# A queue that spreads the transpositions of the attention heads over the long products, and another spacing of the gates in the last attention stage

## The chip, the cores and the metric

One core of a Trainium2 chip runs the whole program. The metric is the device time of one execution in microseconds. The kernel is written with a tile scheduler: the code names tiles and operations, and the scheduler then puts the instructions of each engine in an order, takes buffers from small pools and adds the waits. An instruction that the code emits earlier has the higher priority; it is placed as soon as the scheduler's own reckoning says that its inputs and buffers are ready.

## What is computed

Two layers on a residual stream of 512 tokens by 1024 columns. Each layer mixes the tokens by five branches of four heads, sums them under gates, projects and normalises; then a mixture of 16 experts follows.

```python
h = x @ w_in                              # all q, k, v of the five branches
o_sb, o_moba, o_mla, o_nsa, o_mem = ...   # five attentions, 4 heads of 64 each, (512, 256) out
for i, o in enumerate((o_sb, o_moba, o_mla, o_nsa, o_mem)):
    gate = sigmoid(x @ w_gate[i] + b_gate[i])       # 1024 x 1024 per branch
    merged = merged + gate * (o @ w_br[i])
h = layer_norm(ALPHA * h + merged @ w_out)
h = layer_norm(ALPHA * h + hierarchical_moe(h))     # 16 experts, two per token
```

Every attention is a softmax over at most 512 keys, but for the stick-breaking one (`sb`), which takes a running product along the keys. The native sparse attention (`nsa`) has two such maps per head (selected and window) and a compressed one.

## The kernel before, in words

Products run in a split form: each operand is a high and a low part, and three products of the parts replace one. So a tile of 128 by 512 out of 1024 inputs is 24 products of 512 columns (`fm_tile`, L166), which the text calls long products.

An attention head is a chain for each of its four query blocks of 128 rows. `score_block` multiplies q by k into a PSUM tile `s` (2 banks, L116); VectorE subtracts the distance and takes the minimum (L254) or only the minimum (L257); ScalarE takes the exponent (L259); VectorE inverts the sum and scales (L260, L262, L264). The result lies in an SBUF tile `ne`, of which there are 3. `to_pt` then turns its blocks of 128 columns on TensorE (`tr`, L124) into a PSUM tile `pt` (2 banks), and ScalarE and VectorE copy them, split, into `pth` and `ptl`. These have one buffer each, so a head's tiles must be read before the next head's are written. When four query blocks have been turned, the product with v follows (`causal_pv`, into the one `pv` bank), then the head's output `oo`. A branch's output is split to `oh`, and `gates` uses it. In `sb` the chain from `s` to `ne` is tanh, a running product (L432) and a difference (L433).

`mixer` runs five stages, one for each branch. In each, `weave` draws from up to three generators, in the order that a string gives: `a` is the next score block (or the end of a head), `g` the next half of a gate tile of the branch before (24 long products, or 6 with `w_br`), `q` the next piece of the next branch's q, k and v. When the string is at its end, what is left of each generator runs. After the last stage the gates of the last branch follow alone, and then the output projection and the experts, whose weights are loaded into memory that the attention's tiles have left.

Before, a step `a` emits the score products and, right behind them, the transpositions of the same block, one after another; the end of a head emits its product with v at once. The scheduler keeps that priority: it places the one to four transpositions of a block together, at the moment when its own reckoning says that the softmax is done.

Of the kernel before, what the change touches and what calls it, by code (L numbers as in the profile page):

```python
# [18 lines left out]
P = 128  # L19
# [51 lines left out]
class Trunk:  # L71
    def __init__(self, tc, A, C, out, dbg=None, upto=None):
        self.tc, self.nc, self.A, self.C, self.out = tc, tc.nc, A, C, out
        self.dbg, self.upto = dbg or {}, upto
        self.uid = 0

    def nm(self, s):
        self.uid += 1
# [33 lines left out]
            return e.tensor_tensor(out, in_, hi.bitcast(F32), ALU.subtract)  # L112
        return e.scalar_tensor_tensor(out, in_, scale, hi.bitcast(F32), ALU.mult, ALU.subtract)

    def mm(self, out, lhsT, rhs, start, stop):
        self.nc.tensor.matmul(out, lhsT, rhs, start=start, stop=stop)  # L116

    def mm3(self, out, ah, al, bh, bl, start, stop):
        self.mm(out, ah, bh, start, False)
# [39 lines left out]
    def fm_tile(self, wh, wl, M=P, N=S, x=None, cut=1):  # L159
        o = self.ps("f")  # L160
        xh, xl = (self.xh, self.xl) if x is None else x
        for c in range(cut):
            n = slice(c * N // cut, (c + 1) * N // cut)
            for k in range(KT):
                for m, (a, b) in enumerate(((wh, xh), (wh, xl), (wl, xh))):
                    self.nc.tensor.matmul(o[:M, n], a[:, k, :M], b[:, k, n], start=c + k + m == 0, stop=k == KT - 1 and m == 2,  # L166
                                          skip_group_check=cut > 1)
        return o

    def fm_chunk(self, w, c0, use, n=2, cut=1):  # L170
# [6 lines left out]
    def tm_chunk(self, w, c0, use, x=None, nt=NT, outer="k"):  # L177

        xh, xl = (self.xh, self.xl) if x is None else x
        o = [self.ps("f") for _ in range(nt // 2)]  # L180
        hl = {}

        def part(g, kk, t):
            if g not in hl:
                hl[g] = self.split_w(self.load_w(w[512 * g : 512 * g + 512, c0 : c0 + 256].rearrange("(k p) c -> p k c", p=P), (4, 256)))
            h, l = hl[g]
            k = 4 * g + kk
            sl = slice(t * P, (t + 1) * P)
            d = o[t // 2][:, 256 * (t % 2) : 256 * (t % 2) + 256]
            for m, (a, b) in enumerate(((xh, h), (xh, l), (xl, h))):  # L190

                self.nc.tensor.matmul(d, a[:, k, sl], b[:, kk, :], start=k == 0 and m == 0 and t % 2 == 0,  # L192
                                      stop=k == KT - 1 and m == 2, skip_group_check=True)
# [72 lines left out]

    def to_pt(self, e, nb, dst):

        t = self.ps("pt")
        for b in range(nb):  # L270
            self.tr(t[:, b * P : (b + 1) * P], e[:, b * P : (b + 1) * P])
        src = t[:, : nb * P].rearrange("p (b q) -> p b q", q=P)
        h, l = dst
        self.hi(h, src)
        self.lo(l, src, h)

    def pv_out(self, pv, o32, at):

# [36 lines left out]
    def causal_head(self, passes, vt, strip=0, slope=1.0):  # L315
        pt = self.pt_tiles()
        for i in range(NT):
            L = P * (i + 1)
            e = self.score_block(i, L, passes, self.strip[:, 384 - P * i : 512] if strip == 0 else None, slope, causal=strip == 1)
            self.to_pt(e, i + 1, self.causal_dst(pt, i))  # L320
            yield
        pv = self.ps("pv")
        self.causal_pv(pv, pt, vt, True, True)
        return pv

    def std_passes(self, q, k):

# [45 lines left out]
    def mem_att(self, l, out):  # L373
        for pr in range(2):
            o32 = self.o_tile()
            out.append(o32)
            for hh in range(2):
                h = 2 * pr + hh
                q, k = self.mq[h], self.mk[h]
                pt = self.pt_tiles()  # L380
                for i in range(NT):
                    e = self.score_block(i, MEM, self.std_passes(q, k), None)
                    self.to_pt(e, 2, [t.rearrange("p (c q) -> p c q", q=P)[:, i : i + 5 : 4, :] for t in pt])
                    yield
                pv = self.ps("pv")
                for j in range(2):
                    for m in range(2):
                        self.mm(pv[:, :S], self.mv[j][:, h, :], pt[m][:, 512 * j : 512 * j + 512], j == 0 and m == 0, j == 1 and m == 1)
                self.pv_out(pv, o32, self.H2[hh])
                yield  # L390
            self.dump(f"o_mem{pr}_{l}", o32)

# [17 lines left out]
    def sb_att(self, l, out):  # L410
        nc = self.nc
        for pr in range(2):
            o32 = self.o_tile()
            out.append(o32)
            for hh in range(2):
                h = 2 * pr + hh
                passes = self.std_passes(self.sq[h], self.sk[h])
                pt = self.pt_tiles()
                for i in range(NT):
                    L = P * (i + 1)  # L420
                    s = self.ps("s")
# [12 lines left out]
                    self.to_pt(t, i + 1, self.causal_dst(pt, i))  # L434
                    yield
                pv = self.ps("pv")
                self.causal_pv(pv, pt, lambda j: self.sv[j][:, h, :], True, True)
                self.pv_out(pv, o32, self.H2[hh])
                yield
            self.dump(f"o_sb{pr}_{l}", o32)  # L440

# [14 lines left out]
    def moba_att(self, l, out):  # L456
        for pr in range(2):
            o32 = self.o_tile()
            out.append(o32)
            for hh in range(2):  # L460
                h = 2 * pr + hh
                q, k = self.bq[h], self.bk[h]
                pv = yield from self.causal_head(self.std_passes(q, k), lambda j: self.bv[j][:, h, :], 0, SLOPES[h])
                self.pv_out(pv, o32, self.H2[hh])
                yield
            self.dump(f"o_moba{pr}_{l}", o32)

# [131 lines left out]
    def mla_att(self, l, out):  # L599
        for pr in range(2):  # L600
            o32 = self.o_tile()
            out.append(o32)
            for hh in range(2):
# [6 lines left out]
                pv = yield from self.causal_head(passes, lambda j: self.lv[j][:, h, :], 1)  # L610
                self.pv_out(pv, o32, self.H2[hh])
                yield
            self.dump(f"o_mla{pr}_{l}", o32)

# [104 lines left out]
    def nsa_att(self, l, out):  # L719
# [32 lines left out]
        for pr in range(2):  # L752
            o32 = self.o_tile()
            out.append(o32)
            for hh in range(2):
# [3 lines left out]
                for m in range(2):  # L759
# [7 lines left out]
                pv = self.ps("pv")  # L767
                self.mm(pv, self.vc[:, h, :], pc[:, 0, :], True, False)
                self.mm(pv, self.vc[:, h, :], pc[:, 1, :], False, False)
                for m in range(2):  # L770
                    self.causal_pv(pv, pts[m], lambda j, m=m: self.nv[j][:, m, :], False, m == 1)
                self.pv_out(pv, o32, self.H2[hh])
                yield
            self.dump(f"o_nsa{pr}_{l}", o32)

# [87 lines left out]
            self.hi(h, v)  # L863
            self.lo(self.xl[:, 4 * g : 4 * g + 4, t * P : (t + 1) * P], v, h)

    @staticmethod
    def weave(parts, order):

        for c in order:
            next(parts[c], None)  # L870
        for g in parts.values():
            for _ in g:
                pass

    def start(self, l):

# [719 lines left out]
    def layer(self, l, gat, att):  # L1596
# [8 lines left out]
        with tc.tile_pool(name=f"pre{l}", bufs=1, reuse_waits="tile") as pre:  # L1605
# [6 lines left out]
            with tc.tile_pool(name=f"exp{l}", bufs=1, reuse_waits="tile") as ep:  # L1612
# [30 lines left out]
    qs = "pp"  # L1643
    wq = "ssss"
    rest = 3
    orders = ('aaaqaaaaqaaaaaaaaaaaaqqa', 'gggqqgaaaaggaaaaaaggaaaaqqggggggaqqqqagagaaa', 'qaagaaggagqqaggaaaqaggaqaaaaqggaqqaaaaggqggqqggqq', 'ggqgaaaaaaaaaaagqgaaaggqagggggggqqqqgaaaaga', 'ggaaaaaaaaaggggggggaaaaaaaaaaaaaaaagaaaaaaaaaagggagg')
    x1 = 0

    class _Pool:
# [66 lines left out]
```

## Time and profile before

| | |
|---|---|
| runs | 1702.87, 1696.06, 1697.85 us; median 1697.85 us |
| profiled execution | 1704.54 us, of which the span of instructions is 1702.7 us |
| mean granted TensorE clock | 0.972 of full speed |
| busy share of the span | TensorE 94%, VectorE 74%, ScalarE 51%, GpSimd 16% |
| attention stages | about 45 to 530 us (layer 0) and 885 to 1385 us (layer 1) |

The profiled execution is a little slower than the runs; its rows are used for durations and for who waits. A busy share of TensorE says little by itself, since products overlap: a product of 512 columns is listed with about 0.4 us, but the next starts 0.23 us after it. Where TensorE has to wait, the listed idle time starts only when the last listed product has ended, so a wait costs that overlap on top of the idle time shown.

### The profile page before, as it was taken

What the parts mean: (1) busy time and instruction counts of PE and PEld (TensorE: products, weight loads), DVE (VectorE), ACT (ScalarE), POOL (GpSimd) and SP (SyncE); (2) the same over time, 40 slices, a digit from 0 to 9 for tenths busy, and PEclk for the clock granted to TensorE, in tenths of its full rate; (3) what the DMA queues carried; (4) which work ended last, traced back from release to release, by engine and by line L of the source; (5) the groups of instructions that cost most, each with busy time, mean ns of one, the idle gap of its engine ahead of it and who ended that gap; (6) DMA issues with size and microseconds to landing.
All of it is one profiled execution on the core that took longest, in us unless ns stands there. A gap on an engine that the chain in (4) does not pass through costs nothing. (4 is left out here: it accounts for less than half of the span.)

```text
span 1702.7 us, 22755 instructions
## 1 busy us (share of the span) xinstructions
PE 1603.2 (94%) x7936; PEld 1271.8 (75%) x7936; DVE 1253.3 (74%) x2551; ACT 867.3 (51%) x1655; POOL 272.7 (16%) x218
## 2 busy tenths in 40 slices
PE   8999999999999998899699999999999999989995
PEld 7877877788777786666587778777877787766673
DVE  6777658764785689988788766588557956898887
ACT  5644446343463335788346444464344624358871
POOL 0000011111112112333300000111101121223332
PEclk9999999989999998999799999999999999999997
DMA  8232222434328747997541323223332285499954
GB/s 254 64 91 77 67 71 61 119 95 124 106 79 281 255 165 282 378 379 251 195 141 52 94 73 81 66 62 98 79 88 63 58 305 183 170 326 380 381 178 156
DMA packets 254563, 273.61 MB, mean 161 GB/s; under 512 B 38666, under 2 KB 191360, under 8 KB 254432
## 3 DMA queue, kind: packets, MB, share of 16 engines
q1 hardware_dynamic: 241032, 223.98, 41.3%
q0 software_dynamic: 13312, 47.98, 8.2%
q8 instruction: 67, 1.10, 0.3%
q14 instruction: 64, 0.52, 0.1%
q10 hardware_dynamic: 88, 0.03, 0.0%
HBM read 239.18 MB, written 32.77 MB: 160 GB/s over the span
## 5 line engine op out<-in xcount | busy, mean ns | idle before, releaser
L166 PE MATMUL f<-xh,wh 128*128 128x512 f32 (+2 forms) x1920 | 631.0, 397 | 2.0 <-DVE ot L592 1.1
L166 PEld LDWEIGHTS f<-xh,wh 128*128 128x128 f32 (+1 forms) x1920 | 355.7, 189 | 77.0 <-PE f L625 1.2
L166 PE MATMUL f<-xl,wh 128*128 128x512 f32 (+2 forms) x960 | 381.1, 397 | 0.0
L112 DVE TENSOR_TENSOR wh<-rw,wh 128x1024 fp32r<-128x1024 f32 (+1 forms) x174 | 227.5, 1313 | 51.5 <-ACT wh L97 50.4
L798 POOL TENSOR_TENSOR mg<-mg,gt 128x512 f32<-128x512 f32 x64 | 96.8, 1512 | 986.1 <-DVE gt L797 986.1
L166 PEld LDWEIGHTS f<-xl,wh 128*128 128x128 f32 (+1 forms) x960 | 181.0, 188 | 36.7 <-DVE xl L112 0.2
L97 ACT CAST wh<-rw 128x1024 fp32r<-128x1024 f32 (+3 forms) x178 | 178.5, 1012 | 52.6 <-PE f L192 14.9
L788 ACT ACTIVATE gt<-f,bgh 128x512 f32<-128x512 f32 x80 | 55.0, 688 | 211.8 <-PE f L166 211.8
L116 PE MATMUL f<-wh,xh 128*112 128x512 f32 (+1 forms) x564 | 153.9, 400 | 1.9 <-DVE wh L112 1.9
L116 PE MATMUL f<-oh,bh 128*128 128x512 f32 x480 | 132.5, 403 | 0.1
L797 DVE SCALAR_TENSOR_TENSOR gt<-gt,f 128x512 f32<-128x512 f32 x64 | 43.8, 684 | 107.3 <-PE f L116 102.8
L116 PEld LDWEIGHTS f<-wh,xh 128*112 128x112 f32 (+1 forms) x564 | 98.3, 178 | 31.8 <-DVE wh L112 3.3
L97 ACT CAST pth<-pt 128x128 fp32r<-128x128 f32 (+1 forms) x192 | 77.4, 417 | 87.2 <-PE pt L124 81.5
L116 PE MATMUL f<-eh,xh 128*112 128x512 f32 (+1 forms) x396 | 110.5, 401 | 0.9 <-DVE eh L112 0.8
L112 DVE TENSOR_TENSOR ptl<-pt,pth 128x128 fp32r<-128x128 f32 (+1 forms) x192 | 88.9, 473 | 24.7 <-ACT pth L97 21.8
L116 PEld LDWEIGHTS f<-oh,bh 128*128 128x128 f32 x480 | 89.8, 191 | 20.0 <-issue 1.2
L116 PE MATMUL s<-qk,qk 128*128 128x256 f32 (+7 forms) x416 | 99.2, 336 | 5.9 <-DVE st L254 2.6
L97 ACT CAST wh<-rp 128x1024 fp32r<-128x1024 f32 x84 | 87.5, 1053 | 30.9 <-PE pt L116 16.3
L112 DVE TENSOR_TENSOR wh<-rp,wh 128x1024 fp32r<-128x1024 f32 x70 | 95.4, 1374 | 8.4 <-ACT wh L97 7.8
L124 PE MATMUL pt<-ident,ne 128*128 128x128 f32 x472 | 83.7, 279 | 8.6 <-DVE ne L433 3.8
L116 PEld LDWEIGHTS s<-qk,qk 128*128 128x128 f32 (+1 forms) x416 | 67.5, 194 | 26.9 <-DVE st L254 9.3
L124 PEld LDWEIGHTS pt<-ident,ne 128*128 128x128 f32 x472 | 54.7, 141 | 42.4 <-issue 17.1
(355 smaller groups left out, 2756.4 us busy)
## 6 DMA issues: line engine op xcount, KB each, us to landing
rp<-in_w_up_dram SPq DMA_DIRECT2D x96, 512.0 KB, 14.4
rw<-in_w_gate_dram SPq DMA_DIRECT2D x80, 512.0 KB, 3.8
rp<-in_w_down_dram SPq DMA_DIRECT2D x48, 512.0 KB, 13.6
rw<-in_w_in_dram SPq DMA_DIRECT2D x38, 512.0 KB, 3.8
rw<-in_w_out_dram SPq DMA_DIRECT2D x32, 512.0 KB, 6.5
yd<-xl POOLq DMA_DIRECT2D x28, 448.0 KB, 6.8
xl<-xd POOLq DMA_DIRECT2D x24, 448.0 KB, 7.5
rb<-in_w_br_dram SPq DMA_DIRECT2D x80, 128.0 KB, 3.3
```

Source lines behind the costliest of these rows:

```text
L97: return nc.scalar.copy(out, in_)
L112: return e.tensor_tensor(out, in_, hi.bitcast(F32), ALU.subtract)
L116: self.nc.tensor.matmul(out, lhsT, rhs, start=start, stop=stop)
L124: return self.nc.tensor.transpose(out, in_, self.ident[:k, :k])
L166: self.nc.tensor.matmul(o[:M, n], a[:, k, :M], b[:, k, n], start=c + k + m == 0, stop=k == KT - 1 and m == 2, skip_group_check=cut > 1)
L788: nc.scalar.activation(t, gp, AF.Tanh, bias=self.bgh[:, b * 8 + f : b * 8 + f + 1], scale=0.5)
L797: nc.vector.scalar_tensor_tensor(t, t, 1.0, bp, ALU.add, ALU.mult)
L798: i = nc.gpsimd.tensor_tensor(m, m, t, ALU.add)
```

## The change

`mm` gets a counter: each product of 256 columns or more is a tick. Emission of the turned blocks goes through a queue (`pend`). `to_pt` puts one entry for each block in it; the first may run 20 ticks after it was queued, each following one 2 ticks after the one before, and after the last of a block row there is a gap that fills up to 10 ticks. The entry of the last block also emits the copies into `pth` and `ptl`. The end of a head, with its product with v, is an entry of the same queue, so it comes behind its own transpositions. `tick` runs inside whatever emits long products at that time, so the blocks are emitted singly between the products of gates and projections. `weave` empties the queue at the end of each stage. All products of `fm_tile` and `tm_chunk` now go through `mm`. The fifth order string is another: its sixteen `g` stood in five clusters of 1 to 8; now they stand in pairs with four or five `a` between them.

```diff
+        self.pend, self.now, self.due, self.big = [], 0, 0, None
...
-    def mm(self, out, lhsT, rhs, start, stop):
-        self.nc.tensor.matmul(out, lhsT, rhs, start=start, stop=stop)
+    def mm(self, out, lhsT, rhs, start, stop, **kw):
+        i = self.nc.tensor.matmul(out, lhsT, rhs, start=start, stop=stop, **kw)
+        if rhs.shape[-1] >= self.long:
+            self.big = i
+            self.tick()
+
+
+    def tick(self):
+
+        if self.busy:
+            return
+        self.now += 1
+        while self.pend and max(self.pend[0][0], self.due) <= self.now:
+            if self.do_next():
+                break
+
+    def do_next(self):
+        _, gap, f = self.pend.pop(0)
+        self.busy = True
+        f()
+        self.busy = False
+        self.due = self.now + gap
+        return gap
+
+    def flush(self):
+        while self.pend:
+            self.do_next()
+
+    def later(self, f, gap=0, delay=0):
+
+        self.pend.append((self.now + delay, gap, f))
...
-        t = self.ps("pt")
+        h, l = dst
+        ts = []
+
+        def turn(b):
+            if b == 0:
+                ts.append(self.ps("pt"))
+            t = ts[0]
+            if True:
+                self.tr(t[:, b * P : (b + 1) * P], e[:, b * P : (b + 1) * P])
+            if b == nb - 1:
+                src = t[:, : nb * P].rearrange("p (b q) -> p b q", q=P)
+                self.hi(h, src)
+                self.lo(l, src, h)
         for b in range(nb):
-            self.tr(t[:, b * P : (b + 1) * P], e[:, b * P : (b + 1) * P])
-        src = t[:, : nb * P].rearrange("p (b q) -> p b q", q=P)
-        h, l = dst
-        self.hi(h, src)
-        self.lo(l, src, h)
+            self.later(lambda b=b: turn(b), self.space if b < nb - 1 else max(1, self.gap_t - self.space * (nb - 1)), 0 if b else self.delay)
...
-        pv = self.ps("pv")
-        self.causal_pv(pv, pt, vt, True, True)
-        return pv
+
+        def out(use):
+            pv = self.ps("pv")
+            self.causal_pv(pv, pt, vt, True, True)
+            use(pv)
+        return lambda use: self.later(lambda: out(use))
...
         for g in parts.values():
             for _ in g:
                 pass
+        self.flush()
...
+    busy = False
+    long, delay, space, gap_t = 256, 20, 2, 10
```

The fifth string, before and now:

```text
ggaaaaaaaaaggggggggaaaaaaaaaaaaaaaagaaaaaaaaaagggagg
ggaaaaaggaaaaggaaaaaggaaaaggaaaaaggaaaaggaaaaaggaaaa
```

What the scheduler makes of it is seen in the order of TensorE's instructions. In both programs 472 blocks of the `ne` tiles are turned. Before, they stand in 178 runs, 36 of which are a single transposition; now they stand in 324 runs, 262 of them single.

The first place is on TensorE in layer 0's MoBA stage (`s` is a score, `pt<-ident,ne` a turned block, `f<-xh,wh` and `f<-xl,wh` long products, `f<-oh,bh` the six products with `w_br`). Before:

```order
L166 MATMUL f_2145<-xh_102,wh_2142 128x512 x2
L166 MATMUL f_2145<-xl_103,wh_2142 128x512
L166 MATMUL f_2145<-xh_102,wh_2142 128x512
L124 MATMUL pt_2104<-ident,ne_2098 128x128 x3
L166 MATMUL f_2145<-xh_102,wh_2142 128x512
L166 MATMUL f_2145<-xl_103,wh_2142 128x512
L124 MATMUL pt_2119<-ident,ne_2113 128x128 x4
L166 MATMUL f_2145<-xh_102,wh_2142 128x512 x2
```

Seventeen long products and three transpositions stand between the score of `ne_2113` and its four transpositions. The same score's blocks now (its score is `s_2099`, its blocks are `ne_2104`; L117 and L154 are the new numbers of L116, L166 and L124):

```order
L117 MATMUL f_2132<-xh_102,wh_2129 128x512 x2
L154 MATMUL pt_2161<-ident,ne_2104 128x128
L117 MATMUL f_2132<-xl_103,wh_2129 128x512
L117 MATMUL f_2132<-xh_102,wh_2129 128x512
L154 MATMUL pt_2161<-ident,ne_2104 128x128
L117 MATMUL f_2168<-oh_2043,bh_2124 128x512 x2
L154 MATMUL pt_2161<-ident,ne_2104 128x128
L117 MATMUL f_2168<-oh_2043,bh_2124 128x512
L117 MATMUL f_2168<-oh_2046,bh_2124 128x512
L154 MATMUL pt_2161<-ident,ne_2104 128x128
```

The four blocks stand two long products apart, and 28 long products and five other transpositions stand between the score and the first of them.

The second place is on TensorE in layer 0's last stage (`nsa`), at the first two scores of the second head; that of 256 columns is the one to look at. Before:

```order
L166 MATMUL f_4407<-xh_102,wh_4404 128x512
L116 MATMUL f_4434<-oh_4015,bh_4399 128x512 x3
L116 MATMUL f_4434<-oh_4018,bh_4399 128x512 x3
L116 MATMUL s_4446<-qk_3754,qk_3849 128x128
L116 MATMUL s_4446<-qk_3755,qk_3849 128x128
L116 MATMUL s_4459<-qk_3754,qk_3849 128x256
L116 MATMUL s_4459<-qk_3755,qk_3849 128x256
```

Now:

```order
L154 MATMUL pt_4281<-ident,ne_4139 128x128
L117 MATMUL f_4296<-oh_4015,bh_4248 128x512 x3
L117 MATMUL f_4296<-oh_4018,bh_4248 128x512
L154 MATMUL pt_4301<-ident,ne_4150 128x128
L117 MATMUL f_4296<-oh_4018,bh_4248 128x512 x2
L117 MATMUL s_4312<-qk_3754,qk_3849 128x128
L117 MATMUL s_4312<-qk_3755,qk_3849 128x128
L117 MATMUL s_4321<-qk_3754,qk_3849 128x256
L117 MATMUL s_4321<-qk_3755,qk_3849 128x256
```

The score `s_4321` takes the PSUM bank of `s_4234`. VectorE's reduction of `s_4234` writes the `ne` buffer that held `ne_4150`, and so it waits for the transposition `pt_4301<-ident,ne_4150`, which now stands two long products and two short ones ahead of the score.

## Rows read from the trace of the kernel before

**Rows 1.** Windows of both attention stretches: length, then busy us by engine.
```profile
45.00:530.00 485.00, 474.91 (x2352) 380.30 (x2352) 334.73 (x774) 236.00 (x530) 49.47 (x42) 0.99 0.33 92
885.00:1385.00 500.00, 491.08 (x2453) 393.78 (x2452) 345.83 (x785) 242.35 (x540) 42.74 (x27) 0.99 0.30 84
```

**Rows 2.** Waits of TensorE: waiting line, releaser, total us, times, longest.
```profile
PE pt L124 <- DVE ne L433: 3.8, 12, 0.5
PE pt L124 <- DVE ne L262: 2.8, 6, 0.8
PE s L116 <- DVE st L254: 2.6, 6, 0.8
PE s L116 <- ACT ne L259: 1.7, 2, 1.4
PE s L116 <- ACT ne L427: 0.8, 2, 0.4
PE pt L124 <- DVE st L260: 0.6, 2, 0.3
PE pt L124 <- DVE ne L264: 0.4, 2, 0.3
```

**Rows 3.** Timeline of TensorE in MoBA: start, us, engine, line, tiles, count, idle.
```profile
213.85 0.39 PE L166 MATMUL f<-xl,wh 128*128 128x512 f32 x1
215.03 0.63 PE L124 MATMUL pt<-ident,ne 128*128 128x128 f32 x4 [0.80 <-DVE ne L262]
```

**Rows 4.** Timeline of VectorE and GpSimd ahead of that wait.
```profile
210.02 0.69 DVE L254 CUSTOM_DVE_ANT_0 ne<-s,strip 128x512 f32<-128x512 f32 x1
...
212.81 1.40 POOL L798 TENSOR_TENSOR mg<-mg,gt 128x512 f32<-128x512 f32 x1 [212.38 <-DVE gt L797]
213.05 1.44 DVE L112 TENSOR_TENSOR bh<-rb,bh 128x256 fp32r<-128x256 f32 x1
214.41 0.47 DVE L262 TENSOR_SCALAR ne<-ne,st 128x512 f32<-128x512 f32 x1
```

**Rows 5.** Timeline of TensorE: one transposition between long products.
```profile
961.80 0.39 PE L166 MATMUL f<-xh,wh 128*128 128x512 f32 x1
962.03 0.27 PE L124 MATMUL pt<-ident,ne 128*128 128x128 f32 x1
962.06 0.48 PE L166 MATMUL f<-xh,wh 128*128 128x512 f32 x1
962.38 0.39 PE L166 MATMUL f<-xl,wh 128*128 128x512 f32 x1
```

**Rows 6.** Timeline of TensorE: four transpositions in a run that waited for nothing.
```profile
280.29 0.40 PE L166 MATMUL f<-xh,wh 128*128 128x512 f32 x1
280.53 0.60 PE L124 MATMUL pt<-ident,ne 128*128 128x128 f32 x4
...
281.20 0.39 PE L166 MATMUL f<-xl,wh 128*128 128x512 f32 x1
```

**Rows 7.** Timeline of TensorE in the latent stage: a score that waited.
```profile
340.39 0.79 PE L116 MATMUL s<-qk,qk 96*128 96x384 f32 x3 [1.42 <-ACT ne L259]
```

**Rows 8.** Groups by form: products with a branch's output.
```profile
L116 PE MATMUL f<-oh,bh 128*128 128x512 f32 x480 | 132.5, 403 | 0.1
```

**Rows 9.** Windows around a fall of the clock; the third last number is the clock.
```profile
360.00:363.00 3.00, 3.00 (x30) 3.00 (x28) 1.14 (x1) 1.62 (x2) 0.00 (x0) 1.00 0.02 3
363.00:366.00 3.00, 3.00 (x13) 2.68 (x13) 0.92 (x6) 0.52 (x4) 0.00 (x0) 0.53 1.10 219
...
369.00:373.00 4.00, 4.00 (x10) 3.14 (x11) 2.22 (x9) 1.91 (x9) 0.36 (x1) 0.50 0.04 8
```

**Rows 10.** Timeline: loads after the attention, and the output projection's first products.
```profile
518.01 1.82 SPq L1329 DMA_DIRECT2D rp<-in_w_up_dram  x3
...
554.45 6.31 SPq L137 DMA_DIRECT2D rw<-in_w_out_dram  x2
...
577.91 0.97 PE L116 MATMUL f<-wh,xh 128*128 128x512 f32 x3
```

More of the change, by code (lines that the diff above doesn't have):

```diff
@@ L165, in fm_tile @@
                 for m, (a, b) in enumerate(((wh, xh), (wh, xl), (wl, xh))):
-                    self.nc.tensor.matmul(o[:M, n], a[:, k, :M], b[:, k, n], start=c + k + m == 0, stop=k == KT - 1 and m == 2,
-                                          skip_group_check=cut > 1)
+                    self.mm(o[:M, n], a[:, k, :M], b[:, k, n], c + k + m == 0, k == KT - 1 and m == 2, skip_group_check=cut > 1)
         return o
@@ L190, in part @@
             for m, (a, b) in enumerate(((xh, h), (xh, l), (xl, h))):
-                self.nc.tensor.matmul(d, a[:, k, sl], b[:, kk, :], start=k == 0 and m == 0 and t % 2 == 0,
-                                      stop=k == KT - 1 and m == 2, skip_group_check=True)
+                self.mm(d, a[:, k, sl], b[:, kk, :], k == 0 and m == 0 and t % 2 == 0, k == KT - 1 and m == 2, skip_group_check=True)
         its = [(g, kk) for g in range(2) for kk in range(4)]
@@ L384, in mem_att, with end @@
                     yield
[L385 to L389, printed above, removed]
+                def end(h=h, hh=hh, pt=pt, o32=o32):
+                    pv = self.ps("pv")
+                    for j in range(2):
+                        for m in range(2):
+                            self.mm(pv[:, :S], self.mv[j][:, h, :], pt[m][:, 512 * j : 512 * j + 512], j == 0 and m == 0, j == 1 and m == 1)
+                    self.pv_out(pv, o32, self.H2[hh])
+                self.later(end)
                 yield
@@ L435, in sb_att, with end @@
                     yield
-                pv = self.ps("pv")
-                self.causal_pv(pv, pt, lambda j: self.sv[j][:, h, :], True, True)
-                self.pv_out(pv, o32, self.H2[hh])
+                def end(h=h, hh=hh, pt=pt, o32=o32):
+                    pv = self.ps("pv")
+                    self.causal_pv(pv, pt, lambda j: self.sv[j][:, h, :], True, True)
+                    self.pv_out(pv, o32, self.H2[hh])
+                self.later(end)
                 yield
@@ L462, in moba_att @@
                 q, k = self.bq[h], self.bk[h]
-                pv = yield from self.causal_head(self.std_passes(q, k), lambda j: self.bv[j][:, h, :], 0, SLOPES[h])
-                self.pv_out(pv, o32, self.H2[hh])
+                pv = yield from self.causal_head(self.std_passes(q, k), lambda j, h=h: self.bv[j][:, h, :], 0, SLOPES[h])
+                pv(lambda x, o32=o32, hh=hh: self.pv_out(x, o32, self.H2[hh]))
                 yield
@@ L609, in mla_att @@
                           (lambda sl: qb[K, sl], lambda sl: ka[K, sl])]
-                pv = yield from self.causal_head(passes, lambda j: self.lv[j][:, h, :], 1)
-                self.pv_out(pv, o32, self.H2[hh])
+                pv = yield from self.causal_head(passes, lambda j, h=h: self.lv[j][:, h, :], 1)
+                pv(lambda x, o32=o32, hh=hh: self.pv_out(x, o32, self.H2[hh]))
                 yield
@@ L766, in nsa_att, with end @@
                     pts.append(pt)
[L767 to L772, printed above, removed]
+                def end(h=h, hh=hh, pts=pts, o32=o32):
+                    pv = self.ps("pv")
+                    self.mm(pv, self.vc[:, h, :], pc[:, 0, :], True, False)
+                    self.mm(pv, self.vc[:, h, :], pc[:, 1, :], False, False)
+                    for m in range(2):
+                        self.causal_pv(pv, pts[m], lambda j, m=m: self.nv[j][:, m, :], False, m == 1)
+                    self.pv_out(pv, o32, self.H2[hh])
+                self.later(end)
                 yield
@@ L864, in x_tile, with weave @@
             self.lo(self.xl[:, 4 * g : 4 * g + 4, t * P : (t + 1) * P], v, h)
-    @staticmethod
-    def weave(parts, order):
+    def weave(self, parts, order):
         for c in order:
@@ L1645 @@
     rest = 3
-    orders = ('aaaqaaaaqaaaaaaaaaaaaqqa', 'gggqqgaaaaggaaaaaaggaaaaqqggggggaqqqqagagaaa', 'qaagaaggagqqaggaaaqaggaqaaaaqggaqqaaaaggqggqqggqq', 'ggqgaaaaaaaaaaagqgaaaggqagggggggqqqqgaaaaga', 'ggaaaaaaaaaggggggggaaaaaaaaaaaaaaaagaaaaaaaaaagggagg')
+    orders = ('aaaqaaaaqaaaaaaaaaaaaqqa', 'gggqqgaaaaggaaaaaaggaaaaqqggggggaqqqqagagaaa', 'qaagaaggagqqaggaaaqaggaqaaaaqggaqqaaaaggqggqqggqq', 'ggqgaaaaaaaaaaagqgaaaggqagggggggqqqqgaaaaga', 'ggaaaaaggaaaaggaaaaaggaaaaggaaaaaggaaaaggaaaaaggaaaa')
     x1 = 0
```

## The prediction

> **What bounds the kernel now.** I read the windows of the two attention stretches first, since the change touches nothing else. TensorE is listed busy for 474.9 of 485 us in layer 0 and for 491.1 of 500 us in layer 1 [rows 1]; VectorE is next, at about 69% in both. So the attention is bound by the rate of TensorE, and all that any new order can win from listed idle time is 10.1 + 8.9 = 19.0 us. Then I read who TensorE waits for. Transpositions (`pt L124`) wait for the end of the softmax: 3.8 + 2.8 + 0.6 + 0.4 = 7.6 us in 22 waits. Scores (`s L116`) wait for a free bank: 2.6 + 1.7 + 0.8 = 5.1 us in 10 waits [rows 2]. A wait costs more than its idle time: a long product is listed with 0.39 us, but the next one starts 0.23 us after it [rows 5], so 0.16 us of overlap is lost as well. One wait shows it: from 213.85 to 215.03 is 1.18 us where 0.23 would do, so 0.95 is lost and 0.80 is shown [rows 3]. With 0.16 for each, transpositions cost 7.6 + 22 x 0.16 = 11.1 us and scores 5.1 + 10 x 0.16 = 6.7 us in the whole program.
>
> The reason for such a wait is a chain that ran slower than it was planned. The score was reduced at 210.02, and its last scaling started at 214.41, because VectorE first had a subtraction for `bh` that took 1.44 us while GpSimd was adding a gate tile [rows 4]. From the start of the score's last product to the first transposition went its own 0.23, 17 long products at 0.23, three transpositions at 0.11 (priced below) and the 0.95 that was lost, together 5.4 us.
>
> **Transpositions singly or in a run.** This is what the change is most visibly about, so I priced it first. One transposition between long products: from 961.80 to 962.38 is 0.58 us, where two long products take 0.46 to 0.47; it adds 0.11 [rows 5]. Four in a run: from 280.29 to 281.20 is 0.91; they add 0.44, which is 0.11 each [rows 6]. So 262 single ones instead of 36 are worth 226 x 0.00 = 0 us. The reason can be seen in the next product's listed 0.48 us: it starts 0.03 us after the transposition but then takes 0.32 until the one after it.
>
> The Trainium skill, on the page "TensorE: Matmul & The Clock Gate" (its opening table of specifications), says that the queue of TensorE is partly reordered, with weight loads pulled ahead of products in flight. By that rule a lone transposition behind a long product would have its weight load covered, and only its own short stream would remain. The rows disagree: two loads fall to one long product there, that of the transposition and that of the product behind it, and the full 0.11 us is paid.
>
> **Waits that go.** The queue moves a transposition away from its score. In the order, counting each product at its pitch in the trace, 138 of 194 block rows had less than 5.4 us of TensorE's work between score and first transposition, the time that the chain took at 215.03; now 35 have. The median distance goes from 4.9 to 8.8 us. At the first place shown under the change there are now 28 long products, 6.4 us, and some transpositions. I take the waits as proportional: 11.1 x 35/138 = 2.8 us remain and 8.3 go. The ends are 11.1 (all go) and 5.5 (half of them have other causes, such as a `pt` bank that is still being copied).
>
> **Waits that come.** A turned block holds its `ne` tile longer, and there are only three. The reduction of a score must wait until its `ne` tile has been turned, and the score after next must wait for the reduction, since there are two banks. In the order, scores that stand less than 1.5 us of TensorE's work behind such a transposition go from 24 to 60. The second place shown is one of them: two long products and two short ones, at most 2 x 0.23 + 2 x 0.11 = 0.68 us, against 0.27 for the transposition [rows 5] and 0.69 for a reduction of 512 columns [rows 4], so 0.28 short. What is queued behind the waiting reduction on VectorE is the other head work and the weights' subtractions; the products that use those are what TensorE would miss next. The lower price is from the waits that can be put on this ring before: `ACT ne L259`, 1.7 + 2 x 0.16 = 2.0 us over 24 places, or 0.08 each, and 36 x 0.08 = 3.0. The upper price is 36 x 0.28 = 10.1; below nothing it can't fall, since a ring that is held longer frees nobody. I take 3.0, as most of the new places are for 128 and 256 columns, where the reduction is shorter and the room just enough.
>
> **What costs nothing, and by which cover.** The branch output's split now comes closer to the products that use it: 2.4 to 2.7 us of TensorE's work from the last product with v in three of five stages, one before. That one stood at 2.4 us and all 480 such products waited 0.1 us in sum [rows 8]; so I price it at nothing, and at 3 us if the cover is gone. The attention's tiles are freed later: the first expert load stands about 12.8 us of TensorE's work later in SP's queue, and the third load for the output projection about 9. In the trace that third load was issued at 554.45 and the projection began at 577.91 [rows 10]; 23 us of room minus 9 still covers it. The gates that were moved in the last stage issue the same loads, casts and adds as before, in pairs; their adds on GpSimd can slow VectorE as at 213.05 [rows 4], but there are no more of them than before.
>
> **The sum.** -8.3 + 3.0 = -5.3 us, 0.3%. The profiled execution took 1704.5 us, so it would be 1699.2 there. The three runs' median is 1697.85, 0.4% less, and on that basis the forecast is 1692.6, rounded to 1693.
>
> **Rivals.** First, the waits go altogether: with the gates spread evenly products are at hand for every stall, and both kinds of waits end, -11.1 - 6.7 = -17.8, that is 1680. For it: VectorE has 30% of its time free. Against it: the `ne` ring is tighter than before. Second, singles are nearly free: only the 0.03 us from the transposition's start to the product's remains of the 0.11, so 226 x 0.08 = 18 us go on top of the 5.3, that is 1675. Against it stand the same shapes in [rows 5, 6]. It is what the Trainium skill's rule above would give. Third, slower: the ring. When the exponent itself writes the `ne` tile, ScalarE stands still with all its casts behind it, and one such score lost 1.42 + 0.16 = 1.58 us [rows 7]. If 11 of the 60 tight places cost that, 17.4 us come and the 8.3 are overrun by more than the 8.5 us that count; with 15 it is -8.3 + 23.7 = +15.4, that is 1713. For it: 60 tight places, half of them within 1 us. Against it: 24 such places before showed this twice. Fourth, waits only change places: TensorE's transpositions no longer wait, but VectorE and ScalarE, whose order is planned on the same reckoning, deliver scores and splits as late as before; 1698. That the change does nothing is ruled out by the order. The falls of the clock, from full to half speed after a string of products of 31 columns [rows 9], stand in the same surroundings in both orders; I count them as unchanged, and a fall that lasts 3 us less or more is worth about 1.5 us, half of it.
>
> **How the numbers follow.** Chances: the forecast 0.50, waits all gone 0.20, singles free 0.04, slower by the ring 0.11, only shifted 0.15. Half a percent, or 8.5 us, is about what a measurement of this kernel can tell from no change, so faster begins below 1689.4 and slower above 1706.3. The forecast's own range is 1697.85 - 11.1 to 1697.85 - 5.5 + 10.1, or 1687 to 1702; about a seventh of it counts as faster. Faster: 0.20 + 0.04 + 0.07 = 0.31. Slower: 0.11 and a little of the forecast's far end, 0.12. The rest, 0.57, is within. The range of 1682 to 1704 leaves out most of the slow case and the better half of the fastest ones.
>
> **What would show it.** In the profile after: `pt L124` waits down from 7.6 to about 2 us; `s L116` waits up from 5.1 to about 8; a lone transposition still adding 0.11 us; listed idle time in the two stretches down from 19 to about 14 us. If transposition waits stay above 5 us, the distance was not what they hung on. If scores wait more than 20 us, the ring decides. If TensorE's pitch itself changes, or the clock falls at new places, the sum was made of the wrong terms.

## The result, and the profile after

The changed kernel took 1715.4 us (median of 6 runs, 1711.7 to 1717.0) against 1698.8 (6 runs, 1695.6 to 1702.9): a ratio of 1.0093 with a 95% interval of 1.0074 to 1.0113. It is 16.6 us slower, outside the range of the prediction. The profiled execution took 1713.6 us with a span of 1711.8.

The profile's page gives TensorE's busy time, before and after:

```profile
PE 1603.2 (94%) x7936; PEld 1271.8 (75%) x7936; DVE 1253.3 (74%) x2551; ACT 867.3 (51%) x1655; POOL 272.7 (16%) x218
PE 1600.7 (94%) x7936; PEld 1263.8 (74%) x7936; DVE 1254.9 (73%) x2551; ACT 869.5 (51%) x1655; POOL 268.2 (16%) x218
```

So TensorE's idle time in the whole program went from 1702.7 - 1603.2 = 99.5 to 1711.8 - 1600.7 = 111.1 us, 11.6 more.

The windows of the two attention stretches (length, then busy us of TensorE, its loads, VectorE, ScalarE, GpSimd, then the clock), the counterpart of [rows 1]:

```profile
45.00:530.00 485.00, 471.17 (x2344) 375.17 (x2342) 336.69 (x769) 235.41 (x527) 49.15 (x41) 0.99 0.32 88
885.00:1385.00 500.00, 486.20 (x2429) 387.87 (x2429) 346.81 (x782) 241.34 (x537) 39.65 (x25) 0.99 0.28 76
```

TensorE is idle for 13.8 + 13.8 = 27.6 us there, where it was 19.0 and was to be 14. That is 8.6 of the 11.6 us. Its waits, the counterpart of [rows 2] (waiting line, releaser, total us, times, longest):

```profile
PE pt L154 <- DVE ptl L113: 6.2, 8, 1.2
PE s L117 <- ACT ne L287: 5.7, 8, 1.4
PE s L117 <- ACT ne L469: 3.3, 6, 0.9
PE pt L154 <- DVE ne L290: 2.4, 2, 1.2
...
PE s L117 <- DVE st L282: 1.3, 3, 0.5
...
PE pt L154 <- DVE ne L475: 0.6, 2, 0.3
PE pt L154 <- DVE st L288: 0.6, 2, 0.3
```

Transpositions now wait 2.4 + 0.6 + 0.6 = 3.6 us for the softmax, half of the 7.6 of before. But they wait 6.2 us for something new, a `pt` bank that has not yet been copied into `ptl`. Scores wait 5.7 + 3.3 + 1.3 = 10.3 us, twice the 5.1 of before, 9.0 of it for the exponent (L287) or `sb`'s tanh (L469), which write an `ne` tile. That the tile was what these were late for is a reading; e4 and e13 below test it.

The place of the longest new wait, in the sparse attention of layer 0 (timeline of TensorE, then of VectorE, ScalarE and GpSimd: start, us, engine, line, tiles, count, idle before):

```profile
464.60 0.63 PE L117 MATMUL pv<-cp,mt 128*128 128x512 f32 x2
465.06 0.40 PE L117 MATMUL pv<-pth,v 128*128 128x512 f32 x1
...
466.17 0.28 PE L117 MATMUL pv<-ptl,v 128*128 128x128 f32 x1
...
466.80 0.40 PE L117 MATMUL f<-xh,wh 128*128 128x512 f32 x1
468.37 1.05 PE L154 MATMUL pt<-ident,ne 128*128 128x128 f32 x7 [1.18 <-DVE ptl L113]
```
```profile
465.81 2.31 DVE L113 TENSOR_TENSOR wh<-rw,wh 128x1024 fp32r<-128x1024 f32 x1
468.04 0.61 DVE L113 TENSOR_TENSOR ptl<-pt,pth 128x128 fp32r<-128x128 f32 x2
```
```profile
466.42 0.54 ACT L98 CAST pth<-pt 128x128 fp32r<-128x128 f32 x2 [1.00 <-PE pv L117]
```
```profile
465.63 1.40 POOL L846 TENSOR_TENSOR mg<-mg,gt 128x512 f32<-128x512 f32 x1 [5.07 <-DVE gt L845]
```

`pth` and `ptl` have one buffer each, and the sparse attention fills them twice a head. The turned rows of the second map stood in both `pt` banks and could not be copied until the sum over the first map had read `pth`, up to 466.4. ScalarE then copied at once. VectorE had meanwhile begun a weight subtraction of 2.31 us, so `ptl` came at 468.04. Seven transpositions stood behind it and then ran as one burst. Before, too, the sum was emitted behind the second map's blocks, and TensorE has no listed wait for `ptl` there; the queue moved it further back, and the blocks came out in a heap.

The gates have a part in this wait. The long subtraction ran beside a GpSimd addition of a gate tile: in this profile the 28 subtractions of this shape that share more than 0.5 us with such an addition average 1.94 us, the 138 others 1.23. With the queue but the old gates (e1 below) the waits for `ptl` are only 1.9 us.

A lone transposition adds what it did (timeline of TensorE, counterpart of [rows 5]): from 335.46 to 336.04 is 0.58 us.

```profile
335.46 0.40 PE L117 MATMUL f<-xh,wh 128*128 128x512 f32 x1
335.69 0.27 PE L154 MATMUL pt<-ident,ne 128*128 128x128 f32 x1
335.72 0.48 PE L117 MATMUL f<-xh,wh 128*128 128x512 f32 x1
336.04 0.39 PE L117 MATMUL f<-xl,wh 128*128 128x512 f32 x1
```

The other part of the loss, by estimate, is the clock. The mean granted clock of the changed kernel's six runs was 0.972, that of the 115 runs of the kernel before beside the experiments 0.977. A thousandth of 1700 us is 1.7 us of full-speed work, so 0.005 is an estimated 8.5 us, if TensorE bounds throughout; between runs of one kernel (283 runs, pooled) a thousandth went with 0.9 us, which would make it 4. With 8.6 us of idle time in the attention that gives 13 to 17 of the 16.6 us, with the 11.6 us of the whole program 16 to 20. The profile of before (0.972, 1704.5 us) was one of its slowest executions, so the two profiles hide this part: in the attention both have 23.9 us at half speed. What remains of TensorE's listed busy time after the half-speed loss is equal: 1603.2 - 0.028 x 1702.7 = 1555.5 us before, 1600.7 - 0.026 x 1711.8 = 1556.2 after.

### The profile page after: what moved, and what is told of

Same layout as the page of the kernel before. It is cut to its first block, busy times and chain, and to the rows that moved or that the text cites. A ratio compares the mean times of both kernels' runs of the same rounds, so it can differ in the third digit from the quotient of the medians.

```text
span 1711.8 us, 22764 instructions
## 1 busy us (share of the span) xinstructions
PE 1600.7 (94%) x7936; PEld 1263.8 (74%) x7936; DVE 1254.9 (73%) x2551; ACT 869.5 (51%) x1655; POOL 268.2 (16%) x218
## 5 line engine op out<-in xcount | busy, mean ns | idle before, releaser
L117 PE MATMUL f<-xh,wh 128*128 128x512 f32 (+2 forms) x1920 | 636.9, 400 | 3.2 <-ACT xh L98 1.2
L117 PEld LDWEIGHTS f<-xh,wh 128*128 128x128 f32 (+1 forms) x1920 | 351.5, 188 | 80.4 <-DVE gt L845 1.5
L117 PE MATMUL f<-xl,wh 128*128 128x512 f32 (+2 forms) x960 | 382.7, 399 | 0.0
L117 PEld LDWEIGHTS f<-xl,wh 128*128 128x128 f32 (+1 forms) x960 | 180.2, 188 | 37.2 <-DVE xl L113 0.2
L117 PE MATMUL f<-wh,xh 128*112 128x512 f32 (+2 forms) x820 | 201.9, 364 | 5.5 <-DVE wh L113 4.1
L98 ACT CAST wh<-rw 128x1024 fp32r<-128x1024 f32 (+3 forms) x178 | 178.9, 1012 | 54.6 <-PE f L117 25.3
L117 PEld LDWEIGHTS f<-wh,xh 128*112 128x112 f32 (+1 forms) x820 | 139.0, 182 | 36.8 <-DVE wh L113 5.9
L117 PE MATMUL f<-oh,bh 128*128 128x512 f32 x480 | 135.1, 408 | 0.4
L154 PE MATMUL pt<-ident,ne 128*128 128x128 f32 x472 | 107.1, 278 | 10.0 <-DVE ptl L113 6.2
L117 PE MATMUL s<-qk,qk 128*128 128x256 f32 (+7 forms) x416 | 102.0, 343 | 11.5 <-ACT ne L287 5.7
L117 PE MATMUL f<-eh,xh 128*112 128x512 f32 (+1 forms) x396 | 109.5, 400 | 0.9 <-DVE eh L113 0.8
L117 PEld LDWEIGHTS f<-oh,bh 128*128 128x128 f32 x480 | 87.1, 191 | 22.8 <-issue 1.2
L117 PEld LDWEIGHTS s<-qk,qk 128*128 128x128 f32 (+1 forms) x416 | 68.1, 195 | 40.6 <-ACT ne L287 15.8
L154 PEld LDWEIGHTS pt<-ident,ne 128*128 128x128 f32 x472 | 61.2, 141 | 35.8 <-DVE ptl L113 11.5
## 6 DMA issues: line engine op xcount, KB each, us to landing
rp<-in_w_down_dram SPq DMA_DIRECT2D x48, 512.0 KB, 13.8
```

The source lines that it names most:

```text
L98: return nc.scalar.copy(out, in_)
L117: i = self.nc.tensor.matmul(out, lhsT, rhs, start=start, stop=stop, **kw)
L154: return self.nc.tensor.transpose(out, in_, self.ident[:k, :k])
```

## The experiments

Theories: **R**, scores wait since the queue holds the three `ne` tiles longer; **V**, the weighted sums behind queued blocks, with one `pth` and one `ptl`; **G**, the respread gates; **S**, lone blocks cost more. A kernel's ratio is to runs of the kernel before on the same chip. "Idle" is TensorE's in the two attention windows of its profile (19.0 us before, 27.6 changed), "all" that of the whole profile (99.5 and 111.1); "clock" is the mean over its timed runs.

| kernel | us | ratio, 95% | idle | all | clock |
|---|---|---|---|---|---|
| e1 queue, old gates | 1715.0 | 1.0098–1.0127 | 25.3 | 108.6 | 0.9725 |
| e2 gates, no queue | 1706.1 | 1.0037–1.0065 | 24.7 | 105.3 | 0.9758 |
| e3 flush at head's end | 1705.2 | 1.0032–1.0062 | 25.2 | 103.9 | 0.9743 |
| e4 six tiles | 1704.9 | 1.0040–1.0066 | 25.2 | 104.5 | 0.9748 |
| e5 blocks together | 1705.4 | 1.0034–1.0069 | 26.0 | 105.9 | 0.9747 |
| e6 flush, six tiles | 1701.5 | 1.0015–1.0037 | 23.9 | 104.4 | 0.9762 |
| e7 before, six tiles | 1695.5 | 0.9977–1.0004 | 18.4 | 99.5 | 0.9779 |
| e8 delay 6 | 1701.5 | 1.0008–1.0041 | 21.7 | 100.5 | 0.9766 |
| e9 as e6, old gates | 1701.6 | 1.0012–1.0031 | 22.2 | 100.5 | 0.9748 |
| e10 delay 6, old gates | 1702.7 | 1.0010–1.0033 | 20.8 | 104.3 | 0.9771 |
| e11 as e10, six tiles | 1694.4 | 0.9971–0.9991 | 17.1 | 99.0 | 0.9783 |
| e12 changed, again | 1712.6 | 1.0069–1.0098 | 28.0 | 109.9 | 0.9738 |
| e13 more tiles | 1705.2 | 1.0030–1.0055 | 26.4 | 111.3 | 0.9758 |
| e14 first map early | 1705.7 | 1.0025–1.0056 | 23.9 | 101.9 | 0.9735 |
| e15 early, more tiles | 1700.6 | 1.0007–1.0027 | 24.8 | 106.7 | 0.9767 |
| e16 as e15, delay 6, old gates | 1699.4 | 0.9996–1.0016 | 19.7 | 103.2 | 0.9770 |
| e17 e11, blocks together | 1697.5 | 0.9988–1.0011 | 19.2 | 98.1 | 0.9755 |
| e18 e11, delay 0 | 1698.9 | 0.9985–1.0015 | 19.7 | 99.4 | 0.9772 |

**The two parts alone.** e1 puts the old string `ggaaaaaaaaagggggggg...` back; e2 is the kernel before with the new one.

> The changed kernel with the last order string of the kernel before: the queue alone, no respread gates. Times so far: before 1698.8 us, changed 1715.4 us, +16.6. Theory V (the head's weighted sum now waits in the queue behind the turned blocks while pth and ptl have one buffer each, so the copies out of the pt banks come late): it is all in the queue, 1712 to 1717. Theory R (the ne ring of 3 is held longer by the queue): also 1712 to 1717. Theory G (the even spread of the gates costs it, since the bunched gates of before came where the sparse attention waited anyway): 1697 to 1703.

> The kernel before with the last order string of the changed one: the respread gates alone, no queue. Theory G: 1710 to 1717. Theories V and R: 1696 to 1701, no difference to the kernel before; a gain of 2 to 4 us would say that the spread covers the sparse attention's waits when the blocks are turned at once.

The queue alone has the whole loss, so G is out as its cause. The gates alone cost 8 to 9 us, which neither V nor R foresaw, but nothing on top of the queue. So the parts don't add. The waits don't either: in e1 those for `ptl` are 1.9 us, where the changed kernel has 6.2 and is no slower, and the scores wait 4.7 + 3.4 + 2.8 = 10.9 us, about as much as there. So V's wait is not what the whole loss hangs on.

```profile
PE pt L154 <- DVE ptl L113: 1.9, 4, 0.7
```

In e2 TensorE waits 3.2 us in the sparse attention of layer 0 (433.4 to 527.1), where it waited 0.8 before. That too few products stood beside the chain there is a reading, not tested:

```profile
PE s L116 <- DVE st L254: 1.7, 3, 1.3
PE pt L124 <- DVE st L260: 1.1, 3, 0.4
PE pt L124 <- DVE ne L264: 0.4, 1, 0.4
```

**Sums and tiles.**

```diff
 # e3, in each head and in causal_head
-                self.later(end)
+                self.flush()
+                end()
 # e4, in score_block; six is set in mla_att, uw stands idle from there on
-        e = self.sb(self.ap, [P, 516], "ne")
+        e = self.sb(self.ap, [P, 512], "uw") if self.six and self.nth % 2 else self.sb(self.ap, [P, 516], "ne")
```

> The changed kernel, but at the end of each head the queue is emptied and the weighted sum is emitted at once, as before; between the blocks of a head the queue stays. Theory V: the sum no longer stands behind queued blocks, 1699 to 1705. Theory R: the blocks of rows 0 to 2 still wait in the queue and hold their ne buffers, only the last row's come sooner; 1709 to 1715.

> The changed kernel, but in the MLA and the sparse attention every other score tile lies in the uw buffers, which stand idle there, so the ring has 6 tiles in place of 3. Theory R: most of the 16.6 us goes, 1700 to 1706, and the PE waits of s tiles for ne go to under 3 us from 11. Theory V: the scores run ahead but the blocks still wait for the copies, 1712 to 1716, with the waits of pt tiles for ptl as before (6 us) or larger.

Each gave back 10 us by the medians, 7 to 8 by the ratios, and each took away the wait that its theory names; but other waits rose. In e3 the waits for `ptl` fell from 6.2 to 1.4 us, while scores waited 7.6 us for the softmax's first reduction (L282) in place of 1.3:

```profile
PE s L117 <- DVE st L282: 7.6, 12, 2.2
...
PE pt L154 <- DVE ptl L113: 1.4, 2, 0.7
```

In e4 the scores' wait for the exponent's tile fell from 5.7 to 0.7 + 0.5 us, that for the reduction rose from 1.3 to 4.0, and the transpositions' for `ptl` hardly moved (waits of the whole program):

```profile
PE pt L154 <- DVE ptl L113: 5.5, 6, 1.1
...
PE s L117 <- DVE st L283: 4.0, 8, 0.9
...
PE s L117 <- ACT ne L473: 3.3, 6, 0.9
...
PE s L117 <- ACT ne L288: 0.7, 4, 0.2
...
PE s L117 <- ACT uw L288: 0.5, 2, 0.2
```

So the attention windows hold only 2.4 us less idle time in either. The whole program holds 7.2 (e3) and 6.6 us (e4) less, and part of that lies in the experts, which no edit touches. There TensorE waits for `sw`, an expert's gated product; the changed kernel, then e5:

```profile
PE pv L154 <- DVE sw L1323: 13.6, 6, 3.4
PE pv L154 <- DVE sw L1323: 9.4, 6, 2.0
```

In every profile the first of these waits in each layer is 3.4 or 1.5 us. It is 3.4 where a weight subtraction on VectorE just ahead takes 3.4 us beside one on GpSimd, and 1.5 where it takes 1.2 (layer 0, VectorE and GpSimd, the changed kernel, then e5):

```profile
656.85 3.37 DVE L113 TENSOR_TENSOR wh<-rp,wh 128x1024 fp32r<-128x1024 f32 x1
656.56 2.58 POOL L113 TENSOR_TENSOR wh<-rp,wh 128x1024 fp32r<-128x1024 f32 x1 [3.78 <-ACT wh L98]
```
```profile
656.14 1.21 DVE L113 TENSOR_TENSOR wh<-rp,wh 128x1024 fp32r<-128x1024 f32 x1
655.55 4.03 POOL L113 TENSOR_TENSOR wh<-rp,wh 128x1024 fp32r<-128x1024 f32 x1 [4.22 <-ACT wh L98]
```

From the start of the experts up to this wait TensorE, VectorE and ScalarE have the same order of work in both kernels. So up to 4 us of a difference between two profiles come from these two places. The kernel before, the changed kernel, e2, e7, e12 and e13 have the long wait in both layers, e5, e8, e11, e14 and e17 in neither, the others in one. Whether the timed runs go with their profile in this is not shown.

**How long the tiles are held.** e5 is `space = 0`, e8 `delay = 6`; e6 joins e3 and e4; e7 has six tiles in the kernel before.

> The changed kernel with space 0 in place of 2: the blocks of a block row still wait 20 long products in the queue, but are then turned one behind the other. Theory S (lone blocks between long products cost more than blocks in a run): the stretch from the first score to the MLA's sums of squares, 163.7 us in every kernel with the queue against 162.5 before, goes back to 162.5, and 1711 to 1713 in all. Theory D (what costs is the delay and the order in the queue, not where a block stands): that stretch stays at 163.7, and 1714 to 1717.

> The changed kernel with both remedies that each took off about 10 us: the queue emptied at each head's end, and six score tiles in the MLA and the sparse attention. If they relieve two different waits (sums behind queued blocks; scores without a tile): 1694 to 1698. If they relieve one chain from two ends: 1702 to 1705, no better than either alone.

> The kernel before with six score tiles in the MLA and the sparse attention. If the ring of 3 holds the scores in the kernel before as well (its waits of s tiles for ne): 1692 to 1695. If it is the queue alone that made the ring short: 1696 to 1698.5, no change.

> The changed kernel with delay 6 in place of 20, so that a block row's first block comes 14 long products (14 x 0.234 = 3.3 us) earlier. If the time that a score tile is held in the queue is what costs: 1706 to 1710 and fewer waits of s tiles for ne. If it is the sums that stand behind the blocks: 1713 to 1717.

Turning a row's later blocks up to 6 products sooner gave 10 us (e5), the first block 14 products sooner gave 14 (e8), better than either theory had it (by the medians). The stretch on which e5's theories parted took 163.0 us, between the two. e5 kept its waits for `ptl` (7.3 us), and 4.2 of its 5.2 us less idle time are the `sw` waits. Both remedies together gave 14 (e6), outside both ranges but nearer to one chain relieved from two ends. The kernel before has no gain clear of noise from more tiles (e7); its ring was not short, or not by much.

**Gates again, the best pair, the changed kernel again.**

> The changed kernel with both remedies (queue emptied at each head's end, six score tiles) and the last order string of before. With the new string it took 1701.5 us. If the 4 us that were left are the spread gates, whose own idle time in the sparse attention was 2.6 us a layer in the run of the gates alone: 1696 to 1699. If they are the lone blocks (1.2 us a layer in the stretch from the first score to the MLA): 1700 to 1703.

> The changed kernel with delay 6 and the last order string of before. With the new string it took 1701.5 us. Theory that the string costs 4 to 5 us whatever the queue does: 1696 to 1698. Theory that the string is needed by the queue, whose sums would else stand among bunched gates: 1702 to 1710, as the queue with delay 20 and the old string (1715) was no better than with the new one.

> Delay 6, the old order string and six score tiles in the MLA and the sparse attention. If the queue with a short delay is worth something in itself (the stretch from the first score to the MLA took 161.5 us with delay 6, 162.5 before, in each layer 1 less), it beats the kernel before with six tiles (1695.5): 1691 to 1695. If not: 1695 to 1698.

> The changed kernel once more, for a second profile beside other kernels on one chip. Theory that about 5 of the 16.6 us are half-speed stretches of the clock (mean granted clock of its runs 0.972 against 0.977 before, and 0.96 us for each 0.001 over all runs so far): 1712 to 1717 at a mean clock of 0.970 to 0.974. If the low clock belonged to the first chip: a mean clock near 0.977 and 1709 to 1712.

The string makes no difference once there is a queue (e9 as e6, e10 as e8). e11 beats both kernels, by 0.19% the one before; it is not clear of e7, which has the six tiles and no queue, and in its profile the `sw` waits are 4.1 us shorter than before, the idle time of the whole program only 0.5. So its gain is not shown to come from the attention. e12 repeats the loss in a second set of runs, with the same `ptl` and `ne` waits in its profile within 0.1 us. Its clock was 0.974, that of the kernel before on the same chip 0.977: an estimated 3 to 6 us of its 14.

**The sum of the first map alone, and all together.** e13 gives more tiles to the memory attention and SB as well; e14 queues the first map's sum before the second map:

```diff
 # e14, in nsa_att, after each map's rows; bank[0] is the head's pv tile
-                    pts.append(pt)
+                    def part(h=h, m=m, pt=pt, bank=bank):
...
+                        self.causal_pv(bank[0], pt, lambda j: self.nv[j][:, m, :], False, m == 1)
+                    self.later(part)
```

> The changed kernel with more score tiles in the memory attention, SB, MLA and the sparse attention (only MoBA keeps 3). With six in MLA and the sparse attention it took 1704.9 us, and scores of SB still waited 3.3 us for ne. Theory R (ring): those go too, 1699 to 1702. Theory V (what is left is the sums behind queued blocks, with one pth and one ptl buffer): 1703.5 to 1706, and the 5.5 us of pt waits for ptl stay.

> The changed kernel, but in the sparse attention the weighted sum of a head's first map is queued right behind that map's turned blocks, and no longer behind those of the second map; the ring stays at 3. Theory V: the pt waits for ptl there, 2.4 us a layer, go: 1705 to 1710. Theory R: nothing changes for the scores, 1711 to 1716.

> Both edits of the two runs before this one in one kernel, with delay 20 and the new order string. If ring and sums together are the whole of the idle time: listed idle near the 99.5 us of before, and 1697 to 1700. If the delay of 20 costs by something else (the clock, the gates): 1702 to 1705.

> As the run before this one, with delay 6 and the order string of before: the version that should beat both kernels. Delay 6, that string and six tiles gave 1694.4 us. If SB's tiles and the early sum add to it: 1690 to 1693. If the waits they take away were covered: 1694 to 1695.

e14 takes the wait of 468.37 away and gives 10 us by the medians, 9 by the ratios, with the ring still at three. Of the 9.2 us less idle time 3.7 lie in the attention windows and 4.3 are the `sw` waits. TensorE's waits in its sparse attention of layer 0 (432 to 528), with none left for `ptl`, which was 2.4 us:

```profile
PE s L117 <- DVE st L282: 1.4, 2, 0.8
PE s L117 <- DVE ne L781: 0.5, 1, 0.5
PE pt L154 <- DVE st L288: 0.3, 1, 0.3
```

More tiles elsewhere added nothing (e13 as e4), and `sb`'s scores still wait 2.9 us for the tanh, 3.3 before that edit; so the ring is the cause for the exponents (e4), but not shown for `sb`:

```profile
PE s L117 <- ACT ne L473: 2.9, 6, 0.6
```

e15 leaves some 3 us, idle time in the windows 5.8 us above the kernel before; over the whole program it is 106.7 us where it was to be near 99.5. e16 missed: with both extras it is 4 to 5 us slower than e11.

Five different edits of the changed kernel (e3, e4, e5, e13, e14) all came to 1704.9 to 1705.7 us. So a rival stands that no run here rules out: its order may be an unlucky one, and almost any other order gives part of the loss back.

**What the idea is worth.**

> The fastest version so far (delay 6, old order string, six tiles in MLA and the sparse attention: 1694.4 us) with space 0 in place of 2, so that a block row's blocks stand together. If lone blocks between long products are worth something in themselves: 1697 to 1700. If they cost or give nothing, as the priced 0.11 us each way says: 1693 to 1696. If they only held the tiles longer: 1691 to 1693.

> The same version with delay 0 in place of 6. If every product of delay only holds tiles: 1691 to 1694. If a delay of some length is what takes the waits of turned blocks for the softmax away: 1696 to 1700, with more pt waits for ne than the 5.9 us of delay 6.

Without lone blocks, or without the delay, no gain over the kernel before is left: 1697.5 and 1698.9. Their intervals touch that of e11, so the difference is small against the noise. In e17 transpositions waited 6.8 us for the softmax's last scaling (`ne L291`), in e11 3.7. In e18 they were to wait longer for the softmax than the 5.9 us of e11 and waited 3.0 + 2.9 = 5.9; so the waits don't show that the short delay is what helped. e11's attention windows, 17.1 us idle:

```profile
45.00:530.00 485.00, 476.25 (x2376) 379.77 (x2375) 334.15 (x772) 237.77 (x532) 47.94 (x41) 1.00 0.33 91
885.00:1385.00 500.00, 491.64 (x2438) 391.88 (x2437) 347.13 (x787) 243.96 (x543) 43.98 (x29) 1.00 0.29 82
```

## Why the prediction was wrong, step by step

- **Singles cost the same (0 us).** Right: 0.58 us for the three starts above, as in [rows 5], and the busy time left after the clock's loss is equal with 36 and with 262 single blocks. The rival of nearly free singles would have shown 18 us here; no run did. The rule that the prediction put beside it is that of the Trainium skill ("TensorE: Matmul & The Clock Gate", opening table), that weight loads are pulled ahead of products in flight. The trace gives the transposition its full 0.11 us even so. e5, with 38 single blocks, has 1596.4 - 0.025 x 1702.3 = 1553.8 us of such busy time, 2 less; so its gain is not the price of a block.
- **Waits that go (-8.3 us).** This is the step that failed. The waits for the softmax fell from 7.6 to 3.6 us, with 0.16 for each from 11.1 to 3.6 + 6 x 0.16 = 4.6, so -6.5. But the blocks got a new last wait, `ptl`, 6.2 + 8 x 0.16 = 7.5 us: 9.8 us of listed waits in all, above the 5 us that the prediction set as its own sign against the distance. It named a bank that is still being copied only as a reason why some waits might stay; it did not ask what the copy waits for. It counted the delayed sum as moved at no cost, though `pth` and `ptl` have one buffer each. e3 and e14, which move the sum forward, bring the wait to 1.4 us each; e1 shows that the respread gates, counted as free, make 6.2 of 1.9.
- **Waits that come (+3.0 us, ends 0 to 10.1).** The mechanism was right for the exponents (e4) and is not shown for `sb`, whose waits for the tanh went from 0.8 to 3.3 us; the size was too small. Scores lost 5.1 + 10 x 0.16 = 6.7 before and 10.3 + 17 x 0.16 = 13.0 after, +6.3, inside the ends. The price per tight place was taken from places that had waited little; the places of the exponent, where [rows 7] showed one, became eight, four in each layer (1.28 us at 339.22).
- **No cost elsewhere.** For the loads right: the first expert load came at 532.93 against 518.01, the third load for the output projection at 563.25 against 554.45, as priced, and the projection at 580.02 found it loaded (issue from SP, then TensorE):

```profile
532.93 0.88 SPq L1377 DMA_DIRECT2D rp<-in_w_up_dram  x2
...
563.25 14.76 SPq L167 DMA_DIRECT2D rw<-in_w_out_dram  x5
```
```profile
580.02 0.97 PE L117 MATMUL f<-wh,xh 128*128 128x512 f32 x3
```

  The split of the branch output gave 0.4 us of listed waits against 0.1 in [rows 8]. For the gates wrong: by themselves they cost 8 to 9 us (e2), and beside the queue they add nothing to the time but bring most of the `ptl` waits (1.9 us in e1).
- **The clock, counted as unchanged.** Wrong by an estimated 4 to 8.5 us, and no term stood for it. The prediction looked at the falls behind the products of 31 columns only; that is two of the sixteen falls in the profile of before, and twelve lie outside the attention. In both profiles of the changed kernel the falls stand about where they stood before, bar one of 3.4 us at 1123 that is new and two of 3.4 us, at 315 and 1162, that are gone. Which falls come more often in the timed runs is not shown, nor by what.
- **The sum.** -6.5 + 7.5 + 6.3 = +7.3 us by waits, 8.6 by listed idle time in the windows, and the clock's part: 12 to 17 of 16.6. The prediction had no term for the 3.0 us of idle time outside the windows. The rival "slower by the ring" (1713) named the right side and one of the mechanisms. That it came near the time is luck: it took 23.7 us from the ring, where scores lost 6.3.

What stays open: why the clock is lower in the timed runs, how the loss divides, and whether another order with the same delay would have been cheaper. e3 to e5 got back 10 us by the medians with 1.6 to 2.4 us of the idle time in the attention windows; their profiles hold 5 to 7 us less over the whole program, 2 to 4 of it in the `sw` waits, and their clock was 0.002 to 0.003 higher. e13 kept all 111 us; in its profile nearly all the gain is the clock, which takes 0.021 x 1701.9 = 36 us there against 0.026 x 1711.8 = 45.

## What to carry to other kernels

Before work is delayed, list every buffer that it holds and every buffer that its consumer must free: a queue in program order puts the consumer behind the delay too, and with one buffer there the producer stands. Keep a delay short against what the ring can hold: 6 long products took 1701.5 us here where 20 took 1715.4. What a short delay is worth over none is not clear of noise (1694.4 and 1698.9 with six tiles). Take the idle time over the whole program, since a wait in a stage that an edit leaves alone can change with it. Compare the clocks of the timed runs as well as those of the profiles.

## What the runs showed of the hardware

The mean granted clock belonged to the order of instructions as much as to the run: 0.972 and 0.974 in two sets of runs of the changed kernel, 0.976 to 0.978 in five sets, on five chips, of the kernel before, with equal products. Kernels with less idle time in the attention mostly had the higher clock (17.1 us and 0.978 in e11, 28.0 and 0.974 in e12), though not all (26.4 and 0.976 in e13, 23.9 and 0.9735 in e14); that waits bring the falls about is not shown.

Work on GpSimd went with slower work on VectorE. In the profile of the changed kernel the weight subtractions of 128x1024 (`wh` from `rw`) took 1.94 us on average beside a gate addition on GpSimd and 1.23 without. The one before `sw` took 3.4 or 1.2 us beside the same subtraction on GpSimd, with the same work ahead of it on TensorE, VectorE and ScalarE, and TensorE then waited 3.4 or 1.5 us.
